# A hybrid decoder trunk on one core: the top-k mixer's probabilities transposed in 32-blocks on VectorE and carried by transfers, instead of 128-blocks on TensorE

## The chip, the core and the metric

The kernel runs on one core of a Trainium2 chip. The metric is the device time of one execution in microseconds (us). Three runs of the kernel before took 1161.17 to 1161.87 us, median 1161.53.

## What is computed

Two layers over a sequence of 512 tokens, 1024 features wide, all in float32. Each layer normalises x, scales and shifts it by a conditioning vector (`mod = silu(c) @ w_ada + b_ada`), projects it with one wide matrix (`z = u @ w_in`), runs three token mixers on parts of z, gates their outputs, projects each back, sums them and adds the result to x:

```
ya = dsa_attention(rope(aq), rope(ak), av, rope(iq), rope(ik), iw)   # "a": top-k attention, 8 heads of 64
yb = swa_sinks_attention(rope(bq), rope(bk), bv, sinks)              # "b": window of 128, 8 query heads, 2 key heads
yc = stick_breaking_attention(cq, ck, cv)                            # "c": 8 heads of 64
merged = sum over b of sigmoid(m_b) * ((y_b * silu(gate_b)) @ w_br_b)
x = x + gate * (merged @ w_out)
```

Mixer a scores all earlier keys with a small indexer, keeps the 128 highest for each query, and takes a softmax of `q k / 8` over those alone: `p = softmax(logits where selected)`, `y = p @ v`. The kernel computes all causal logits and adds a mask of -1e30 where a key is not selected.

## The kernel before, in words

**Layout.** Activations lie feature-major: 128 features on the partitions, 512 tokens along the row. Weights stream from HBM in chunks of 128x512 (256 KB) into `wstage` (4 buffers, lines 706 to 751); each chunk is split into a high part `whi` and a rest `wlo` (a cast and a subtraction, on VectorE, ScalarE or GpSimd), and every product is three matmuls (`uh*whi`, `ul*whi`, `uh*wlo`). One projected tile of 128 features takes 24 of them into one PSUM bank (`ttile`, line 981); there are three such banks (`ps_z`) and five others (`ps_s`).

**Mixers.** Heads go in pairs p = 0 to 3, two heads e to a pair, the 512 queries in four blocks i of 128. For mixer a the steps of a pair are:

- `softmax_qk` (line 1240): logits of the causal blocks into five PSUM banks; VectorE adds the mask and takes the row maximum, writing five `t` buffers of 128x512; ScalarE takes the exponent with the row sum in `den`; then each of the eight (e, i) stretches of 128 to 512 columns is multiplied in place by 1/den, on VectorE or ScalarE (line 1305).
- `softmax_tr` (line 1309): P has queries on the partitions, and the product with V needs keys there. TensorE transposes the 20 causal blocks of 128x128 one by one into five PSUM banks (line 1326), and each bank is copied to another `t` buffer by ScalarE or VectorE (line 1331).
- `softmax_pv` and `value_run` (lines 1335 to 1357): for key block j and head e, V (64 columns) is the weight and the transposed stretch of up to 512 columns is the moving operand; the two heads use the two halves of the array. `finish_pair` (line 1144) multiplies by the gate and splits y into high part and rest.

Mixers b and c use the same steps with 14 and 20 blocks. `RIDE` and `GROUPS` (lines 47, 48) say where the product with V goes: for mixer a, pair 0 goes with the logits of pair 1, pairs 1 and 2 go together after the transposes of pair 2, and pair 3 goes alone.

**Order.** `Weave` (line 81) lays out a first order of all streams, with fixed distances (`SPACE`, line 43; 13.022 us in mixer a from the logits to the transposes of a pair, 0.5 us from there to the product with V). `Recorder` (line 261) then simulates the engines with a price for each instruction (`price`, line 337), lets each instruction go as soon as its operands and buffers are there, picks the engine where there is a choice, and repeats this five times with priorities from the latest allowed start; the best order is emitted as it stands. So every engine, and SP's queue of transfers, runs a fixed order, and an instruction that is late holds up what stands behind it. Beside the mixers runs the filling work: tiles of the projection (`ttile`) and of the branch projections (`branch_item`, line 1419), the latter adding up k = 0 to 3 over the pairs' y. Mixer a is the last of the three; when its pair 3 is under way only the `ma` gate tiles and the first three parts of a branch tile can still go without pair 3's y.

**Buffers.** `SLOTS` (line 152) gives 14 buffers of 128x512 to `t`; `vc`, `vb` and `va` (V of the three mixers) have one buffer each; x and the merged result reuse `vc` and `va`. All transfers but eight are issued by SP; the eight saves of x are issued by ScalarE (line 1502).

Of the kernel before, what the change touches and what calls it, by code (L numbers as in the profile page):

```python
# [25 lines left out]
F32 = mybir.dt.float32  # L26
# [6 lines left out]
S = 512  # L33
P = 128
# [9 lines left out]
QCOST = 2408  # L44
BKEY = "cfree2"
LOAD_AHEAD, SPLIT_AHEAD = 4, 3
RIDE = {('c', 1): (0,), ('c', 2): (1,), ('c', 3): (2,), ('a', 1): (0,)}
GROUPS = {'c': ((3,),), 'a': ((1, 2), (3,)), 'b': ((0, 1), (2, 3))}

# [74 lines left out]
def by_tile(wv, *gens):  # L124
# [6 lines left out]
    while live:  # L131
# [15 lines left out]
        else:  # L147
# [1 line left out]

SLOTS = {"t": 14, "e": 2, "zs": 2, "m2": 2, "zc": 2, "G": 2, "sm": 2, "Y": 5, "Q": 2, "KH": 2, "dot": 2, "dotg": 2,
         "m8": 2, "mx": 2, "nm": 2, "den": 2, "wstage": 4, "whi": 4, "wlo": 4, "ps_z": 3, "ps_s": 5}


# [9 lines left out]
class View:  # L165
# [14 lines left out]
    def rearrange(self, how, a):  # L180
# [2 lines left out]
        at = np.lib.stride_tricks.as_strided(self.at, (n, a, w // a), (self.at.strides[0], self.at.strides[1] * (w // a), self.at.strides[1]))  # L183
        return View(self.tile, self.ops + (("rearrange", how, a),), at, self.dtype)

    def unsqueeze(self, d):
        return self._with(np.expand_dims(self.at, d), self.dtype, "unsqueeze", d)

# [7 lines left out]
    def real(self):  # L196
        ap = self.tile.real()
        for name, arg, *more in self.ops:
            ap = ap.rearrange(arg, a=more[0]) if more else getattr(ap, name)(arg)
        return ap  # L200

    def regions(self):
# [58 lines left out]
class Recorder:  # L261
# [75 lines left out]
    def price(self, x, engine, op, args, kw):  # L337
# [16 lines left out]
        from_psum = any(v.tile.pool.name[:3] == "ps_" for v in x.reads)  # L354
        if engine == "PE":
            if op == "pairs":
                w = [q[2].shape[-1] for q in args]
# [52 lines left out]
    def forward(self):  # L410
# [38 lines left out]
        while len(out) < len(self.list):  # L449
# [51 lines left out]
            if y.mode == "dma":  # L501
                if not x.writes:
                    x.end = at + 2.1
                else:
                    x.end = dma_free = max(at + (2.1 if at < 20.0 else 3.0), dma_free) + y.lag * (1.2 if dma_free < 5.5 else 1.0)
# [121 lines left out]
def trunk(ctx, tc, xT, vecs, w_ss, w_gt, w_first, w_t, w_v, w_br, w_o, rope, consts, out):  # L627
# [272 lines left out]
    def key_and_value(z):  # L900

        zs, m2, zc = t512("zs"), t512("m2"), t512("zc")
        cast(zs, z)
        cast(zc[H0], z[H0])
        SP.dma_start(zc[H1], zs[H0])
        for a, b in ((0, 32), (32, 0), (64, 32), (96, 0)):
            SP.dma_start(m2[a:a + 32], zs[b:b + 32])
        both(zc, zc, cos_t, OP.mult)
        both(m2, m2, sin_t, OP.mult)
        both(zc, zc, m2, OP.add)  # L910
        tb = sbank()
# [328 lines left out]
    def softmax_qk(b, p):  # L1240
        def fn():
# [8 lines left out]
            es = (0, 1)  # L1250
# [34 lines left out]
            for e in range(2):  # L1285
# [14 lines left out]
                DVE.reciprocal(den[:, es], den[:, es])  # L1300
                for i in (3, 2, 1, 0):
                    bk, c0 = pos(e, i)
                    t = pt[bk][:, c0:c0 + keys(b, i)[1]]
                    r = den[:, 4 * e + i:4 * e + i + 1]
                    rec.add({"DVE": ("tensor_scalar", (t, t, r, None), dict(op0=OP.mult)), "ACT": ("activation", (t, t, AF.Copy), dict(scale=r))})
            st["p", p] = pt
        return op(1900 if b == "a" else 1400, fn)

    def softmax_tr(b, p):
        def fn():  # L1310
            pt = st.pop(("p", p))
            pos, tpos = (bpos, btpos) if b == "b" else (apos, cpos)
# [5 lines left out]
            for e in range(2):  # L1318
                for j in range(4):
                    bk, c0 = tpos(e, j)  # L1320
                    if tb[bk] is None:
                        tb[bk] = sbank()
                    for i in (range(j, min(4, j + 2)) if b == "b" else range(j, 4)):
                        sbk, s0 = pos(e, i)
                        kc = s0 + 128 * j - keys(b, i)[0]
                        PE.transpose(tb[bk][:, c0 + 128 * (i - j):c0 + 128 * (i - j) + 128], pt[sbk][:, kc:kc + 128], ident)
                    left[bk] -= 1
                    if not left[bk]:
                        W = 384 if b == "b" and bk >= 2 else 512
# [5 lines left out]
    def value_run(b, ps, bank, quads=()):  # L1335

        quads, ys = list(quads), []
        for p in ps:
# [4 lines left out]
            for j in range(4):  # L1343
                W = min(256, S - 128 * j) if b == "b" else S - 128 * j
                for e in range(2):
                    bk, c0 = tpos(e, j)
                    h = 2 * p + e
                    c = 64 * (h // 4 if b == "b" else h)
                    quads.append((y[64 * e:64 * e + 64, 128 * j:128 * j + W], st["v" + b][:, j, c:c + 64], PT[bk][:, c0:c0 + W], j == 0))
        pairs(quads)  # L1350
        for p, y in ys:
            finish_pair(b, p, y)
# [66 lines left out]
    def branch_item(l, b, d):  # L1419
        def fn(w):  # L1420
# [15 lines left out]
            both(g, g, s, OP.add)  # L1436
            if b == "a":
                if d % 4 == 0:
                    st["mh", d // 4] = rec.tile(("vc", "va")[d // 4], [P, 4, S], F32R)
# [117 lines left out]
    def start():  # L1557
# [18 lines left out]
        xx = [rec.tile(t, [P, 4, S], F32) for t in ("vc", "va")]  # L1576
# [151 lines left out]
```

## Time and profile before

| | |
|---|---|
| median of the runs | 1161.53 us |
| the profiled execution's own time | 1161.48 us |
| its span, first to last instruction | 1159.7 us |
| TensorE busy | 1148.5 us, 99% of the span |
| VectorE, ScalarE, GpSimd busy | 965.7, 550.9, 170.4 us |
| moved by the DMA engines | 139.39 MB, mean 120 GB/s |
| granted TensorE clock, mean | 0.998 |

The profile page has one busy total for each engine, the span cut into 40 slices, the chain of waits that ended last followed back from the end, and groups of like instructions. All recorded instructions carry the line of the helper that emits them (599, or 597 for the pairs of matmuls in half arrays), so a group is told by its tiles: `ps_s<-small,t` is a transpose of a `t` buffer against the identity (`small` holds it), `t<-ps_s` the copy out of PSUM, `m<-zs` the swap of halves for the rotary embedding. Matmuls overlap, so the distance of their starts, and not the duration of one, is what TensorE spends; the chain of waits gives that.

### The profile page before, as it was taken

Reading aid. Unit: us, or ns where it says so; the run is one execution under the profiler, and the core shown is the slowest. Engines: PE = TensorE matmul, PEld = TensorE weight load, DVE = VectorE, ACT = ScalarE, POOL = GpSimd, SP = SyncE. Lnnn points to the kernel's source line nnn. Section 1 sums busy time; section 2 is a strip of 40 time slices with the busy share of each in tenths; the row PEclk is TensorE's granted clock in tenths of the full one; section 3 lists DMA queues with packets and bytes.
Section 4 is the critical chain, followed back from the end, with each engine's and each line's share of the span. In section 5 each row is a group of like instructions: output and inputs, shape, how many; then the busy total and the mean of one; then the engine's idle time right before and its main releaser. Section 6 shows DMA issues by size and latency. Waiting matters only on the chain.

```text
span 1159.7 us, 17599 instructions
## 1 busy us (share of the span) xinstructions
PE 1148.5 (99%) x5891; PEld 960.7 (83%) x5891; DVE 965.7 (83%) x2222; ACT 550.9 (48%) x1165; POOL 170.4 (15%) x221
## 2 busy tenths in 40 slices
PE   8999999999999999999999999999999999999997
PEld 6899887888888887788899988778888888877886
DVE  8967999999898986877687589999998988567765
ACT  5623676753565642432133157674545665232222
POOL 0100355511011100000000015562010010000001
PEclk9999999999999999999999999999999999999999
DMA  9744333344344355346534432334333333223343
GB/s 355 230 118 123 92 84 92 108 118 114 110 111 122 121 149 141 100 128 181 168 115 110 124 108 75 99 91 121 108 100 105 98 90 109 91 82 92 96 123 108
DMA packets 80474, 139.39 MB, mean 120 GB/s; under 512 B 9984, under 2 KB 20480, under 8 KB 80384
## 3 DMA queue, kind: packets, MB, share of 16 engines
q1 hardware_dynamic: 79232, 136.17, 40.4%
q10 hardware_dynamic: 1152, 2.10, 0.5%
q8 instruction: 46, 0.75, 0.3%
q14 instruction: 44, 0.36, 0.1%
HBM read 125.39 MB, written 4.19 MB: 112 GB/s over the span
## 4 chain that ended last, share of the span: by engine, by line
PE 98%; DVE 1%; ACT 0%; DMA 0%; issue 0%; SPq 0%; DVEq 0%
PE ps_z L599 74%; PE ps_s L599 18%; PE ps_s L597 4%; PE ps_z L597 2%; DMA vc<-in_xT 0%; ACT t L599 0%; DVE t L599 0%; DVE Y L599 0%; DVE wlo L599 0%; DVE xm L599 0%; ACT csr L599 0%; ACT zs L599 0%; ACT e L599 0%; DVE whi L599 0%; ACT ps_s L599 0%
## 5 line engine op out<-in xcount | busy, mean ns | idle before, releaser
L599 PE MATMUL ps_z<-uh,whi 128*128 128x512 f32 (+1 forms) x905 | 355.4, 394 | 0.0
L599 PE MATMUL ps_z<-uh,wlo 128*128 128x512 f32 (+1 forms) x905 | 352.2, 390 | 0.0
L599 PE MATMUL ps_z<-ul,whi 128*128 128x512 f32 (+1 forms) x905 | 352.0, 390 | 0.0
L599 DVE TENSOR_TENSOR wlo<-wstage,whi 128x512 fp32r<-128x512 f32 (+2 forms) x292 | 190.9, 657 | 16.2 <-ACT whi L599 6.7
L599 PEld LDWEIGHTS ps_z<-uh,wlo 128*128 128x128 f32 x905 | 170.0, 188 | 34.8 <-issue 0.5
L599 PEld LDWEIGHTS ps_z<-uh,whi 128*128 128x128 f32 x905 | 169.9, 188 | 34.8 <-issue 1.9
L599 PEld LDWEIGHTS ps_z<-ul,whi 128*128 128x128 f32 x905 | 170.0, 188 | 33.0 <-issue 0.3
L599 DVE CAST whi<-wstage 128x512 fp32r<-128x512 f32 (+1 forms) x202 | 82.7, 410 | 122.4 <-PE ps_z L599 101.4
L599 POOL TENSOR_TENSOR wlo<-wstage,whi 128x512 fp32r<-128x512 f32 (+1 forms) x80 | 102.3, 1283 | 367.3 <-ACT whi L599 133.7
L599 ACT CAST whi<-wstage 128x512 fp32r<-128x512 f32 (+2 forms) x129 | 77.2, 603 | 128.5 <-PE ps_z L599 107.2
L599 PE MATMUL ps_z<-Y,whi 128*128 128x512 f32 x384 | 119.2, 391 | 0.0
L599 ACT ACTIVATE e<-ps_z 128x512 f32<-128x512 f32 x68 | 40.4, 594 | 116.9 <-PE ps_z L599 116.6
L599 PEld LDWEIGHTS ps_z<-Y,whi 128*128 128x128 f32 x384 | 71.7, 188 | 14.5
L599 ACT ACTIVATE e<-e 128x512 f32<-128x512 f32 x96 | 59.8, 630 | 34.5 <-DVE e L599 33.8
L599 PE MATMUL ps_z<-Y,wlo 128*128 128x512 f32 x192 | 74.9, 390 | 0.0
L599 ACT ACTIVATE t<-t 128x512 f32<-128x512 f32 x120 | 69.3, 625 | 8.9 <-DVE t L599 8.5
L599 ACT ACTIVATE t<-t,nm 128x256 f32<-128x256 f32 (+3 forms) x128 | 65.1, 510 | 11.5 <-DVE nm L599 11.4
L599 PE MATMUL ps_s<-small,t 128*128 128x128 f32 x432 | 57.3, 273 | 0.0
L599 PEld LDWEIGHTS ps_s<-small,t 128*128 128x128 f32 x432 | 50.2, 140 | 7.8 <-ACT t L599 1.6
L599 DVE MAX8 m<-score 128x8 f32<-128x256 f32 (+2 forms) x96 | 53.1, 555 | 1.3
L599 DVE MATCH_REPLACE8 score<-m,score 128x256 f32<-128x256 f32 (+2 forms) x96 | 52.1, 543 | 0.1
L599 PE MATMUL ps_s<-wlo,uh 128*128 128x364 f32 x144 | 47.5, 330 | 0.0
(218 smaller groups left out, 1950.6 us busy)
## 6 DMA issues: line engine op xcount, KB each, us to landing
wstage<-in_w_t SPq DMA_DIRECT2D x212, 256.0 KB, 2.7
wstage<-in_w_v SPq DMA_DIRECT2D x48, 182.0 KB, 2.4
m<-zs SPq DMA_DIRECT2D x128, 64.0 KB, 2.0
wstage<-in_w_gt SPq DMA_DIRECT2D x32, 256.0 KB, 2.7
wstage<-in_w_ss SPq DMA_DIRECT2D x32, 256.0 KB, 2.8
wstage<-in_w_o SPq DMA_DIRECT2D x32, 256.0 KB, 2.7
Y<-in_w_ss SPq DMA_DIRECT2D x15, 512.0 KB, 5.8
wstage<-in_w_first SPq DMA_DIRECT2D x16, 256.0 KB, 3.9
```

The lines of the kernel that those rows point to most:

```text
L597: self.real[engine].matmul(*[real(a) for a in q[:3]], start=q[3], stop=True, skip_group_check=True)
L599: made = getattr(self.real[engine], y.op)(*[real(a) for a in y.args], **{k: real(v) for k, v in y.kw.items()})
```

## The change

For mixer a alone (`TR32`), the multiplication by 1/den writes to a new tile `X` of 128x2560 instead of back into `t`. X holds the 20 blocks as four quarters of 640 columns: quarter b has the 32 columns 32b to 32b+31 of every block, so a written stretch falls into runs of 32. VectorE then transposes every 32x32 square of a quarter in place (one instruction of 128x640, four to a pair). After that, square (a, b) of each block holds the right values but sits on partitions 32a instead of 32b; 16 transfers of 32x640 (80 KB) for each pair carry it from X to `U`, issued by SP or ScalarE as the planner picks. The product with V reads its moving operand from U in runs of 32 columns. TensorE's transposes of mixer a and the copies from PSUM go; mixers b and c keep theirs, but their copies now go to one tile `U` of 128x2560.

Buffers: `t` has 5 instead of 14; X and U have one each; `vc` and `vb` become one tile `V5` of 128x2560, whose room also takes the transposed P of pairs 1 and 3 of mixers a and b. Prices: a transfer from SBUF to SBUF now costs SP or ScalarE 0.63 us and another 0.35 (before: 0.58 and 0.36 on SP, 0.1 on ScalarE), and a small one lands after 2.2 instead of 3.0 us.

```diff
+TR32 = {'a': (0, 1, 2, 3)}
-SLOTS = {"t": 14, "e": 2, ...
+SLOTS = {"t": 5, "X": 1, "U": 1, "e": 2, ...
@@ price
-            y.cost, y.lag, y.mode = (0.58 if x.reads and x.writes and not x.reads[0].tile.pool.fixed else 0.36) if engine == "SP" else 0.1, n * 4 / 385e3, "dma"
+            y.cost, y.lag, y.mode = (0.63 if x.reads and x.writes and not x.reads[0].tile.pool.fixed and not o.tile.pool.fixed else 0.35) if engine == "SP" else 1.0 if engine == "POOL" else 0.63 if x.reads and not o.tile.pool.fixed else 0.35, n * 4 / 385e3, "dma"
@@ forward
-                    x.end = dma_free = max(at + (2.1 if at < 20.0 else 3.0), dma_free) + ...
+                    x.end = dma_free = max(at + (2.1 if at < 20.0 else 2.2 if y.lag < 0.22 else 3.0), dma_free) + ...
@@ key_and_value
-        v = st["vb"] = rec.tile("vb", [P, 4, P], F32)
+        st["V5"] = rec.tile("V5", [P, 5 * S], F32)
+        v = st["vb"] = st["V5"][:, 4 * S:].rearrange("p (a b) -> p a b", a=4)
@@ v_phase
-            st["vc"] = rec.tile("vc", [P, 4, S], F32)
+            st["vc"] = st["V5"][:, :4 * S].rearrange("p (a b) -> p a b", a=4)
@@ softmax_qk
-                    t = pt[bk][:, c0:c0 + keys(b, i)[1]]
+                    W = keys(b, i)[1]
+                    t = o = pt[bk][:, c0:c0 + W]
+                    if p in TR32.get(b, ()):
+                        if X is None:
+                            X = rec.tile("X", [P, blocks(b) * P], F32)
+                        o, t = strided(X, b, e, i), t.split((W // P, 4, 32), (0, 1, 2))
-                    rec.add({"DVE": ("tensor_scalar", (t, t, r, None), dict(op0=OP.mult)), "ACT": ...
+                    rec.add({"DVE": ("tensor_scalar", (o, t, r, None), dict(op0=OP.mult)), "ACT": ...
+    def softmax_tr32(b, p):
+        def fn():
+            pt = st.pop(("p", p))
...
+            N = blocks(b)
+            X = pt
+            U = st["V5"][:, :N * P] if p % 2 and b in ('a', 'b') else rec.tile("U", [P, N * P], F32)
+            n = N * 32
+            for b_ in range(4):
+                q = X[:, n * b_:n * b_ + n]
+                DVE.transpose(q, q)
+                for a_ in range(4):
+                    how = ("dma_start", (U[32 * b_:32 * b_ + 32, n * a_:n * a_ + n], X[32 * a_:32 * a_ + 32, n * b_:n * b_ + n]), {})
+                    rec.add({"SP": how, "ACT": how})
+            st["pt", p] = U
@@ softmax_tr (mixers b and c)
-                        PT[bk] = t512("t", 10)
+                        if all(v is None for v in PT):
+                            whole = st["V5"] if b != "c" and p % 2 else rec.tile("U", [P, 5 * S], F32)
+                        PT[bk] = whole[:, S * bk:S * bk + S]
@@ value_run
+                    if p in TR32.get(b, ()):
+                        lo = column(b, e, j)
+                        x = PT.split((4, blocks(b), 32), (1, 0, 2))[:, lo:lo + W // P]
+                        o = o.split((W // P, 4, 32), (0, 1, 2))
+                    else:
+                        x = PT[bk][:, c0:c0 + W]
```

## Rows read from the trace of the kernel before

**Rows 1.** The page: busy time of each engine, then two of the lines of 40 slices (VectorE's busy tenths, and TensorE's granted clock in tenths).
```profile
PE 1148.5 (99%) x5891; PEld 960.7 (83%) x5891; DVE 965.7 (83%) x2222; ACT 550.9 (48%) x1165; POOL 170.4 (15%) x221
...
DVE  8967999999898986877687589999998988567765
...
PEclk9999999999999999999999999999999999999999
```

**Rows 2.** The page: the chain of waits that ended last, by engine.
```profile
PE 98%; DVE 1%; ACT 0%; DMA 0%; issue 0%; SPq 0%; DVEq 0%
```

**Rows 3.** The page's groups: all 128x128 transposes of the three mixers (count, busy us, mean ns of one).
```profile
L599 PE MATMUL ps_s<-small,t 128*128 128x128 f32 x432 | 57.3, 273 | 0.0
```

**Rows 4.** The chain of waits in order of time, first layer, mixer a (start us, us, what, count). `ps_s L599 x20` and the two `x10` are transposes, `L597` x16 and x32 the products with V, `ps_z L599` projection work.
```profile
341.51 16.54 PE ps_z L599 x72
358.05 2.18 PE ps_s L599 x20
...
367.88 2.31 PE ps_z L597 x16
...
386.76 2.18 PE ps_s L599 x20
...
413.13 2.18 PE ps_s L599 x20
...
456.15 4.46 PE ps_s L597 x32
...
474.10 1.09 PE ps_s L599 x10
...
476.58 1.09 PE ps_s L599 x10
...
479.53 2.31 PE ps_s L597 x16
481.83 18.38 PE ps_z L599 x80
```

**Rows 5.** The same chain, second layer: the first and the last of the five pieces of transposes of mixer a.
```profile
926.00 2.18 PE ps_s L599 x20
...
1043.84 1.09 PE ps_s L599 x10
```

**Rows 6.** Busy time by stretch, the stretches of pairs 0, 1 and 2 of mixer a in either layer (stretch: us, then busy us and count of PE, weight loads, DVE, ACT, POOL; granted clock; DMA share; GB/s).
```profile
332.00:360.00 28.00, 28.00 (x159) 22.76 (x157) 25.67 (x64) 17.93 (x40) 2.66 (x4) 1.00 0.41 116
360.00:389.00 29.00, 29.00 (x152) 23.52 (x150) 25.37 (x66) 17.76 (x42) 3.77 (x4) 1.00 0.37 110
389.00:416.00 27.00, 27.00 (x136) 22.71 (x135) 24.91 (x64) 15.64 (x37) 4.89 (x6) 1.00 0.45 134
...
900.00:928.00 28.00, 28.00 (x159) 22.91 (x157) 25.64 (x61) 17.97 (x40) 0.40 (x1) 1.00 0.36 98
928.00:957.00 29.00, 29.00 (x152) 23.51 (x151) 23.84 (x58) 18.08 (x42) 3.20 (x3) 1.00 0.32 89
957.00:984.00 27.00, 27.00 (x136) 22.72 (x135) 23.92 (x57) 16.23 (x38) 1.23 (x2) 1.00 0.38 107
```

**Rows 7.** Groups of instructions in the stretch 332 to 416 us: the copies of transposed blocks out of PSUM (count, busy us, mean ns).
```profile
L599 DVE COPY t<-ps_s 128x512 f32<-128x512 f32 x7 | 4.6, 685 | 0.0
...
L599 ACT COPY t<-ps_s 128x512 f32<-128x512 f32 x8 | 4.4, 579 | 0.0
```

**Rows 8.** Groups of the whole span by shape: VectorE instructions of several widths (count, busy us, mean ns).
```profile
L599 DVE CAST whi<-wstage 128x512 fp32r<-128x512 f32 x158 | 67.3, 427 | 93.8 <-PE ps_z L599 84.1 <-PE ps_s L599 6.5 <-issue 2.4
...
L599 DVE TENSOR_TENSOR_SCAN t<-ps_s,t 128x511 f32<-128x511 f32 x40 | 47.1, 1205 | 0.1
...
L599 DVE COPY t<-ps_s 128x512 f32<-128x512 f32 x33 | 21.7, 682 | 0.1
...
L599 DVE COPY t<-ps_s 128x384 f32<-128x384 f32 x7 | 3.8, 547 | 0.0
```

**Rows 9.** The transfers from SBUF to SBUF that exist: issue on SP's queue (ns min/median/max), and time from issue to landing.
```profile
L599 SPq DMA_DIRECT2D m<-zs x128: 507/583/1627, 55.0 to 974.1; - x128
...
DMA to landing us min/median/max: 1.9/2.0/3.5
```

**Rows 10.** The transfers that ScalarE issues: issue time (ns min/median/max).
```profile
L599 ACTq DMA_DIRECT2D xsave<-xm x8: 326/333/353, 545.1 to 584.7; - x8
```

**Rows 11.** The page's transfers: the weight chunks (count, KB each, median us from issue to landing).
```profile
wstage<-in_w_t SPq DMA_DIRECT2D x212, 256.0 KB, 2.7
```

**Rows 12.** Instructions in order of time at pair 3 of the first layer: VectorE's and ScalarE's last multiplications by 1/den, then TensorE's first matmul after the product with V, and its first one with y of pair 3.
```profile
475.71 0.67 DVE L599 TENSOR_SCALAR t<-t,den 128x384 f32<-128x384 f32 x2
...
475.25 1.02 ACT L599 ACTIVATE t<-t,den 128x512 f32<-128x512 f32 x2
...
481.76 0.50 PE L599 MATMUL ps_z<-uh,wlo 128*128 128x512 f32 x1
...
483.49 0.39 PE L599 MATMUL ps_z<-Y,whi 128*128 128x512 f32 x1
```

**Rows 13.** The same chain of waits in mixer c: the end of pair 0's transposes, and the product with V that goes with the next pair's logits.
```profile
138.06 0.44 PE ps_s L599 x4
...
142.06 2.30 PE ps_z L597 x16
```

**Rows 14.** Instructions in order of time at pair 0 of mixer a, first layer: VectorE's last multiplication by 1/den.
```profile
352.39 0.61 DVE L599 TENSOR_SCALAR t<-t,den 128x384 f32<-128x384 f32 x2
```

More of the change, by code (lines that the diff above doesn't have):

```diff
@@ L148, in by_tile @@
             yield item
-SLOTS = {"t": 14, "e": 2, "zs": 2, "m2": 2, "zc": 2, "G": 2, "sm": 2, "Y": 5, "Q": 2, "KH": 2, "dot": 2, "dotg": 2,
+SLOTS = {"t": 5, "X": 1, "U": 1, "e": 2, "zs": 2, "m2": 2, "zc": 2, "G": 2, "sm": 2, "Y": 5, "Q": 2, "KH": 2, "dot": 2, "dotg": 2,
          "m8": 2, "mx": 2, "nm": 2, "den": 2, "wstage": 4, "whi": 4, "wlo": 4, "ps_z": 3, "ps_s": 5}
@@ L184, in rearrange, with split, quarters @@
         return View(self.tile, self.ops + (("rearrange", how, a),), at, self.dtype)
+    def split(self, sizes, perm):
+        n, w = self.at.shape
+        st_, strides = self.at.strides[1], []
+        for k in range(len(sizes)):
+            strides.append(st_ * int(np.prod(sizes[k + 1:])))
+        at = np.lib.stride_tricks.as_strided(self.at, (n, *sizes), (self.at.strides[0], *strides))
+        return View(self.tile, self.ops + (("split", tuple(sizes), tuple(perm)),), at.transpose(0, *[k + 1 for k in perm]), self.dtype)
+    def quarters(self):
+        n, w = self.at.shape
+        at = np.lib.stride_tricks.as_strided(self.at, (n // 4, 4, w), (self.at.strides[0], self.at.strides[0] * (n // 4), self.at.strides[1]))
+        v = View(self.tile, self.ops + (("quarters", None),), at, self.dtype)
+        v.regions = self.regions
+        return v
     def unsqueeze(self, d):
@@ L198, in real @@
         for name, arg, *more in self.ops:
-            ap = ap.rearrange(arg, a=more[0]) if more else getattr(ap, name)(arg)
+            if name == "quarters":
+                ap = ap.rearrange("(a r) n -> r a n", a=4)
+            elif name == "split":
+                ap = ap.rearrange("p (%s) -> p %s" % (" ".join("abcd"[:len(arg)]), " ".join("abcd"[k] for k in more[0])), **dict(zip("abcd", arg)))
+            else:
+                ap = ap.rearrange(arg, a=more[0]) if more else getattr(ap, name)(arg)
         return ap
@@ L356, in price @@
             if op == "pairs":
-                w = [q[2].shape[-1] for q in args]
+                w = [int(np.prod(q[2].shape[1:])) for q in args]
                 low, full = ([v for v, q in zip(w, args) if (q[2].dtype == F32) == t][::2] for t in (False, True))
@@ L504, in forward @@
                 else:
-                    x.end = dma_free = max(at + (2.1 if at < 20.0 else 3.0), dma_free) + y.lag * (1.2 if dma_free < 5.5 else 1.0)
+                    x.end = dma_free = max(at + (2.1 if at < 20.0 else 2.2 if y.lag < 0.22 else 3.0), dma_free) + y.lag * (1.2 if dma_free < 5.5 else 1.0)
                 lanes.append(x.end)
@@ L1249, in fn @@
             den = rec.tile("den", [P, 8], F32)
-            es = (0, 1)
+            es, X = (0, 1), None
             for i in (3, 2, 0, 1) if b == "a" else (2, 3, 1, 0):
@@ L1302, in fn, with blocks, grid, strip @@
                     bk, c0 = pos(e, i)
-                    t = pt[bk][:, c0:c0 + keys(b, i)[1]]
+                    W = keys(b, i)[1]
[4 more added lines that the diff above has]
+                        o, t = strided(X, b, e, i), t.split((W // P, 4, 32), (0, 1, 2))
                     r = den[:, 4 * e + i:4 * e + i + 1]
-                    rec.add({"DVE": ("tensor_scalar", (t, t, r, None), dict(op0=OP.mult)), "ACT": ("activation", (t, t, AF.Copy), dict(scale=r))})
-            st["p", p] = pt
+                    rec.add({"DVE": ("tensor_scalar", (o, t, r, None), dict(op0=OP.mult)), "ACT": ("activation", (o, t, AF.Copy), dict(scale=r))})
+            st["p", p] = X or pt
         return op(1900 if b == "a" else 1400, fn)
+    def blocks(b):
+        return 14 if b == "b" else 20
+    def grid(X, b):
+        return X.split((4, blocks(b), 32), (1, 0, 2))
+    def strip(b, e, i):
+        if b == "b":
+            return (7 * e + 2 * i - 1, 1, 2) if i else (7 * e, 1, 1)
+        return (i, 3, i + 1) if e == 0 else (16 + i, -4, i + 1)
+    def column(b, e, j):
+        return 7 * e + 2 * j if b == "b" else 4 * j if e == 0 else 16 - 3 * j
+    def strided(X, b, e, i):
+        g0, dg, n = strip(b, e, i)
+        g = grid(X, b)
+        return g[:, g0:(g0 + dg * n if g0 + dg * n >= 0 else None):dg]
+    def softmax_tr32(b, p):
+        def fn():
+            pt = st.pop(("p", p))
+            pos = bpos if b == "b" else apos
+            N = blocks(b)
[9 more added lines that the diff above has]
+            st["pt", p] = U
+        return op(1520 if b == "b" else 2180, fn)
     def softmax_tr(b, p):
+        if p in TR32.get(b, ()):
+            return softmax_tr32(b, p)
         def fn():
@@ L1348, in value_run @@
                     c = 64 * (h // 4 if b == "b" else h)
-                    quads.append((y[64 * e:64 * e + 64, 128 * j:128 * j + W], st["v" + b][:, j, c:c + 64], PT[bk][:, c0:c0 + W], j == 0))
+                    o, x = y[64 * e:64 * e + 64, 128 * j:128 * j + W], None
+                    if p in TR32.get(b, ()):
+                        lo = column(b, e, j)
+                        x = grid(PT, b)[:, lo:lo + W // P]
+                        x = PT.split((4, blocks(b), 32), (1, 0, 2))[:, lo:lo + W // P]
+                        o = o.split((W // P, 4, 32), (0, 1, 2))
+                    else:
+                        x = PT[bk][:, c0:c0 + W]
+                    quads.append((o, st["v" + b][:, j, c:c + 64], x, j == 0))
         pairs(quads)
@@ L1438, in fn @@
                 if d % 4 == 0:
-                    st["mh", d // 4] = rec.tile(("vc", "va")[d // 4], [P, 4, S], F32R)
+                    st["mh", d // 4] = rec.tile("V5", [P, 5 * S], F32R)[:, :4 * S].rearrange("p (a b) -> p a b", a=4) if d == 0 else rec.tile("va", [P, 4, S], F32R)
                 if d % 2 == 0:
@@ L1575, in start @@
         DVE.scalar_tensor_tensor(gb, b_ada[0][:, 8:16], 1.0, g_sb[0], op0=OP.add, op1=OP.mult)
-        xx = [rec.tile(t, [P, 4, S], F32) for t in ("vc", "va")]
+        xx = [rec.tile("V5", [P, 5 * S], F32)[:, :4 * S].rearrange("p (a b) -> p a b", a=4), rec.tile("va", [P, 4, S], F32)]
         x = st["x"] = [xx[k // 4][:, k % 4] for k in range(KT)]
```

## The prediction

> **What bounds the kernel now.** I read the busy totals first, then the chain of waits, then the stretches around mixer a. TensorE is busy 1148.5 of 1159.7 us and its granted clock is in the top tenth all through [rows 1]; the chain that ends last is TensorE for 98% [rows 2]. So a microsecond of TensorE work taken away is one of the end, unless TensorE then waits. The next engine is VectorE at 83% on average, but at nine tenths in many slices [rows 1]: in the stretches of pairs 0 to 2 of mixer a it is busy 75.95 of 84 us in the first layer and 73.40 of 84 in the second, with ScalarE at 51.3 and 52.3 and GpSimd at 11.3 and 4.8 [rows 6]. Mixer a runs in TensorE's shadow except at one place. Pair 0's stretches are all normalised at 353.0 us [rows 14], its transposes stand at 358.05 and its product with V at 367.88; pairs 1 and 2 are multiplied only at 456.15 [rows 4]. Pair 3 alone is tight: normalised at 476.4 [rows 12], multiplied at 479.53 [rows 4].
>
> **What goes.** A duration of 273 ns for a transpose [rows 3] is not its price, since they overlap. The chain has the 20 transposes of a pair as one piece of 2.18 us, or two of 1.09, in both layers [rows 4, 5]: 0.109 us each, and 8 x 2.18 = 17.4 us for eight pairs. That is the gain at most, up to some tenths for the change of mode around them. The Trainium skill (TensorE: Matmul & The Clock Gate, Part 4: PE-mode transpose) gives about 275 ns for a transpose in a kernel and says that the full clock doesn't engage for them. By its figure the term would be 160 x 0.275 = 44 us (an estimate); the trace has the same duration but 0.109 us from start to start, and a granted clock of 1.00 in the stretches that hold them [rows 6], so I do not take it.
>
> The 40 copies from PSUM go too: in pairs 0 to 2 of the first layer 7 on VectorE and 8 on ScalarE, 4.6 and 4.4 us [rows 7]. None is on the chain; what they give is room.
>
> **What comes, on VectorE.** Per pair four 32-block transposes of 128x640, which no row shows. Lower end: the fast cast of 427 ns for 512 columns [rows 8], scaled to 640, 0.53 us. Upper end: the scan's 1.205 us for 511 columns [rows 8], 1.51 us. I take one element per step, as the copies from PSUM have it: 547 ns for 384 and 682 for 512 [rows 8], so 135 ns per 128 and 0.82 us for 640; less the 0.08 by which neighbours overlap there, 0.74. Four make 2.95 us a pair. The strided multiplications by 1/den keep their columns; between no cost and the loss of their fast form (2560 columns a pair, at 1.05 instead of some 0.5 ns: 1.4 us if all are VectorE's) I take none, their rows being still runs of 32.
>
> VectorE's demand in the three stretches of the first layer is then 75.95 + 3 x 2.95 - 4.6 = 80.2 us, in a time of 84 - 3 x 2.18 = 77.5: more than fits. The planner can hand normalisations and weight casts to ScalarE, which holds 51.3 - 4.4 us there plus the transfers it issues (below: 24 x 0.58 = 14), 61 of 77.5. So at least 3 us of work must move, and a little will be late: I take 1 us of TensorE idle per layer, 2 us in all; the ends are nothing, and the rival below.
>
> **What comes, on the queues.** 16 transfers of 80 KB a pair, 128 in all. The nearest rows are the rotary swaps of 64 KB: 0.58 us of issue, landed 2.0 after it began [rows 9]. Sixteen cost 9.3 us of issue on one queue, 4.7 on two. ScalarE's own issues take 0.33 [rows 10], but those go to HBM; I use 0.58 for both. For pairs 0 to 2 this is covered: from 353.0 us, 2.95 of transposes, 9.3 of issue and 2.0 of landing, even end to end, reach 367.3, the product's old place being 367.88. That cover is thin with TensorE earlier, but other projection work can go first there; pairs 1 and 2 have 40 us.
>
> **Pair 3.** Old distance from last normalisation to product: 476.4 to 479.53. New: first transpose done at 477.2; 16 issues on two queues start their last at 481.3, landed 483.3; on one queue 477.2 + 15 x 0.58 + 2.0 = 487.9. The product is 3.8 to 8.4 us later, and TensorE is there 2.2 earlier: 6.0 to 10.6 us to cover. Behind the product lie 18.4 us of projection work [rows 4], which starts at 481.76, with y needed from 483.49 [rows 12]. Of it 19 matmuls of the next gate tile at 0.23 (16.54/72, rows 4), 9 of the next branch tile and 12 of the gate tile after can go ahead, 9.2 us, if PSUM banks and weights are there. So on two queues it is covered, and on one not quite. I take 0.75 us per layer, 1.5 in all (ends: 0; 16, see the rival).
>
> **The rest, at nothing.** Five `t` buffers: mixer c's are read by its transposes until 138.5 us, and the next pair writes only after its logits, beside the product at 142.06 [rows 13]; without that gap each late pair would cost its wait. U and V5 are written by a pair's copies after the product of their earlier tenant, or late V has been read; if that order were broken the copies, and TensorE's banks behind them, would wait. Strided moving rows in the product with V: from nothing to a second pass over its 2 x (2.31 + 4.46 + 2.31) = 18.2 us [rows 4]; I take nothing, as columns and weights stay the same. The new prices make a new order everywhere; I leave that at 2 us either way.
>
> **Sum.** -17.4 + 2.0 + 1.5 = -13.9 on the profiled execution's 1161.48 us, 0.05 below the median: 1147.6.
>
> **Rivals.**
> *VectorE becomes the bound.* If little is handed over and VectorE can be filled to 95%, the six stretches need 80.2/0.95 = 84.4 and, with as many copies in the second layer, (73.40 + 8.85 - 4.6)/0.95 = 81.7 us: they gain 1.9 together instead of 13.1. With the two pairs 3 (-4.4 + 1.5) that gives -4.8, 1156.7. For it: the 90% of rows 6. Against: ScalarE's and GpSimd's idle share. The Trainium skill (VectorE: DVE Perf Modes, Rules for kernel authors) advises TensorE for a 128x128 transpose whose result may go to PSUM; that is this rival's side, and the trace speaks against the rule where TensorE is the bound, for it where VectorE is.
>
> *Pair 3 is not covered.* If only the 19 matmuls (4.3 us) can move, two queues leave 6.0 + 1.7 (from product to y) - 4.3 = 3.4 us a layer, one queue 8.0. Then -17.4 + 2 + 6.8 = -8.6, 1152.9; at worst 1162. For it: y of pair 3 gates every later branch tile. Against: the 9.2 us above.
>
> *Slower: SP's queue holds up the weights.* A burst stands in SP's fixed order in front of weight chunks, and waits there for VectorE. TensorE eats a chunk of 12 matmuls in 2.76 us [rows 4]; four ahead make 11.0, less 2.7 to land [rows 11] and 1.1 to split (0.43 for the cast and 0.68 for a subtraction at one element per step, rows 8), 7.2 of cover. If SP issues all sixteen unbroken, with 0.74 of wait, it is shut for 10.0 us: 2.8 of stall at each of eight bursts, 22.4 against 17.4, so +5.0 with nothing else: 1166.5. It decides from a shut time of 7.2 + 2.2 = 9.4 us a burst. For it: 9.3 us of issue. Against: ScalarE shares them, and the planner can put loads between.
>
> **Chances.** Forecast 0.55, VectorE 0.17, pair 3 0.13, SP's queue 0.15. About 0.2% (2.3 us) is what a measurement of this kernel tells from no change. Of the VectorE case 0.03, of pair 3 0.02 and of SP's queue 0.02 fall within that: faster 0.80, same 0.07, slower 0.13. The range: low, the whole 17.4 and 2 of the new order, 1142; high 1160.5, which takes in VectorE's case and pair 3's but for its worst. The forecast's own range is 1143 to 1151.
>
> **What would show it.** Right: no `ps_s<-small,t` of mixer a (432 down to 272), TensorE's busy time down by some 17 us, its idle time up by under 5; VectorE's transposes near 0.82 us; the products of pairs 0 to 2 free of waits. VectorE's rival: idle of TensorE on `whi` or `wlo` from VectorE in 330 to 410 and 900 to 980. Pair 3's: a gap of over 3 us before its product or before the first matmul with its y. SP's: weight loads queued behind transfers, and waits on `wstage`. I am wrong if TensorE's busy time falls by 17 and the span doesn't follow for a reason in none of these, or if the products with V lengthen.

## The result, and the profile of the changed kernel

The changed kernel takes 1145.95 us (median; 1145.84 to 1146.28) against 1161.70 (1161.17 to 1162.05) for the kernel before in the same rounds: ratio 0.9865, 95% interval 0.9848 to 0.9882. The profiled execution took 1145.84 us with a span of 1144.0, so 15.7 us of span have gone. The lines of helpers are L620 and L618 now instead of L599 and L597.

The page: busy time, two of the lines of 40 slices, and the chain by engine.
```profile
PE 1133.1 (99%) x5731; PEld 943.6 (82%) x5731; DVE 985.9 (86%) x2254; ACT 541.3 (47%) x1140; POOL 144.1 (13%) x206
...
DVE  8977999999999987887686589999999999767765
...
PEclk9999999999999999999999999999999999999999
...
PE 92%; DVE 5%; DMA 1%; issue 1%; ACT 0%; SPq 0%; DVEq 0%; ACTq 0%
```
Against [rows 1], TensorE has 160 matmuls fewer and 15.4 us less of busy time, and its clock has not moved: the span fell by what TensorE no longer does. VectorE has 20 us more and GpSimd 26 less; more of VectorE's slices stand at nine tenths. In the chain VectorE went from 1% [rows 2] to 5%.

TensorE's transposes (groups by shape: count, busy us, mean ns).
```profile
L620 PE MATMUL ps_s<-small,t 128*128 128x128 f32 x272 | 38.1, 273 | 0.1
```
What reads or writes X, by operation (ns min/median/max, first and last start); `V` is the tile V5, and the last line is for the transfers.
```profile
L620 SPq DMA_DIRECT2D U<-X x37: 507/586/1329, 356.5 to 983.2; - x37
L620 ACTq DMA_DIRECT2D V<-X x36: 514/530/689, 389.2 to 1035.8; - x36
L620 DVE STREAM_TRANSPOSE X<-X x32: 799/822/846, 355.6 to 1033.2; 128x640 f32<-128x640 f32 x32
L620 SPq DMA_DIRECT2D V<-X x28: 507/592/818, 389.2 to 1036.2; - x28
L620 ACTq DMA_DIRECT2D U<-X x27: 514/552/1529, 356.5 to 980.4; - x27
...
DMA to landing us min/median/max: 2.0/2.5/5.2
```
432 transposes [rows 3] are 272. SP issues 65 of the 128 transfers, ScalarE 63, at 0.53 to 0.59 us each.

Two stretches that answer to [rows 6] (us, then busy us and count of PE, weight loads, DVE, ACT, POOL; granted clock; DMA share; GB/s): pairs 0 to 2 in either layer.
```profile
333.00:413.00 80.00, 79.32 (x390) 63.89 (x389) 77.25 (x190) 45.85 (x105) 7.29 (x6) 1.00 0.52 155
893.00:971.00 78.00, 78.00 (x385) 62.96 (x385) 72.92 (x174) 42.93 (x98) 8.40 (x7) 1.00 0.48 135
```
VectorE went from 90% to 97% in the first layer. There, and there alone, TensorE stands for 0.68 us.

The chain of waits in order of time, first layer, mixer a; with [rows 4], what stands where the pieces of 2.18 and 1.09 us stood.
```profile
342.50 13.83 PE ps_z L620 x60
356.36 0.07 DVE X L620
...
361.60 0.84 DVE X L620
...
363.02 0.75 DVE X L620
...
365.88 0.61 DVE zc L620
...
366.53 4.15 PE ps_z L620 x17
...
371.45 2.31 PE ps_z L618 x16
...
421.92 4.46 PE ps_s L618 x32
...
460.95 19.54 PE ps_z L620 x84
480.49 2.30 PE ps_s L618 x16
482.80 17.23 PE ps_z L620 x75
```
Three things are to be seen. No piece of transposes is left, and the products with V take 2.31, 4.46 and 2.30 us as before. At 356 to 366 us the chain runs through VectorE, one instruction behind the other, all four transposes of pair 0's X among them; it ends at `zc`, a product for the rotary embedding that reads a projected tile out of PSUM, for which the next tile waited: TensorE stood 0.68 us and restarted with gaps, 0.9 in all. And pair 3 has no wait at all: one piece of projection work of 19.54 us ends where its product begins.

**Where the 15.7 us lie.** Starts of the same work in both traces: the projection block that the chain shows at 55.44 us before starts at 56.20 after, 0.76 late. Mixer a's first logits move from 339.35 to 340.33, the second layer's first block from 623.29 to 616.48, its first logits of mixer a from 907.29 to 900.62, the end from 1159.7 to 1144.0. The two stages that hold mixer a give 7.79 (from +0.98 to -6.81) and 9.03 (from -6.67 to -15.70), where four pairs of 2.18 are 8.72: the first is short by the 0.9 us of the wait, the second is 0.3 above. The stages ahead of them lose 0.98 and 0.14, most of it at the start. There, VectorE's order has changed. VectorE in order of time, the kernel before:
```profile
16.88 0.76 DVE L599 TENSOR_TENSOR ul<-e,uh 128x256 fp32r<-128x256 f32 x2
17.55 1.22 DVE L599 SCALAR_TENSOR_TENSOR Y<-Y,csr 128x1024 f32<-128x1024 f32 x1
```
The same moment in the changed kernel:
```profile
16.60 1.21 DVE L620 SCALAR_TENSOR_TENSOR Y<-Y,csr 128x1024 f32<-128x1024 f32 x1
...
17.74 0.41 DVE L620 TENSOR_TENSOR ul<-e,uh 128x256 fp32r<-128x256 f32 x1
```
The planner put a dot product of 1.2 us (`Y<-Y,csr`, for the conditioning) ahead of `ul`, and TensorE waits for `ul`, here and once more at 50.9 us: 0.16 us of idle time each, but 0.44 and 0.55 us from one start to the next where 0.12 and 0.23 are usual, together 0.64 of the 0.76.

### The profile page after: what moved, and what is told of

The parts are those of the page before. It is cut to its first block, busy times and chain, and to the rows that moved or that the text cites. A ratio compares the mean times of both kernels' runs of the same rounds, so it can differ in the third digit from the quotient of the medians.

```text
span 1144.0 us, 17545 instructions
## 1 busy us (share of the span) xinstructions
PE 1133.1 (99%) x5731; PEld 943.6 (82%) x5731; DVE 985.9 (86%) x2254; ACT 541.3 (47%) x1140; POOL 144.1 (13%) x206
## 4 chain that ended last, share of the span: by engine, by line
PE 92%; DVE 5%; DMA 1%; issue 1%; ACT 0%; SPq 0%; DVEq 0%; ACTq 0%
PE ps_z L620 71%; PE ps_s L620 15%; PE ps_s L618 4%; DVE t L620 2%; PE ps_z L618 1%; DVE wlo L620 1%; DMA Y<-in_w_ss 1%; DVE Y L620 1%; DMA wstage<-in_w_first 0%; DVE Q L620 0%; SPq L620 0%; DVE ps_s L620 0%; DVE X L620 0%; DVE V L620 0%; DVE m L620 0%
## 5 line engine op out<-in xcount | busy, mean ns | idle before, releaser
L620 PE MATMUL ps_z<-uh,whi 128*128 128x512 f32 (+1 forms) x905 | 354.2, 393 | 0.7 <-DVE zc L620 0.7
L620 PE MATMUL ps_z<-ul,whi 128*128 128x512 f32 (+1 forms) x905 | 352.5, 390 | 0.3 <-DVE ul L620 0.3
L620 PE MATMUL ps_z<-uh,wlo 128*128 128x512 f32 (+1 forms) x905 | 351.4, 389 | 0.0
L620 DVE TENSOR_TENSOR wlo<-wstage,whi 128x512 fp32r<-128x512 f32 (+2 forms) x328 | 215.7, 659 | 11.1 <-ACT whi L620 3.6
L620 PEld LDWEIGHTS ps_z<-uh,whi 128*128 128x128 f32 x905 | 169.8, 188 | 35.7 <-issue 1.4
L620 PEld LDWEIGHTS ps_z<-ul,whi 128*128 128x128 f32 x905 | 169.9, 188 | 34.3 <-issue 1.0
L620 PEld LDWEIGHTS ps_z<-uh,wlo 128*128 128x128 f32 x905 | 169.9, 188 | 34.2 <-issue 0.3
L620 DVE CAST whi<-wstage 128x512 fp32r<-128x512 f32 (+2 forms) x198 | 80.6, 408 | 86.9 <-PE ps_z L620 68.3
L620 ACT CAST whi<-wstage 128x512 fp32r<-128x512 f32 (+2 forms) x132 | 79.2, 602 | 111.6 <-PE ps_z L620 89.8
L620 PE MATMUL ps_z<-Y,whi 128*128 128x512 f32 x384 | 118.7, 390 | 0.0
L620 ACT ACTIVATE e<-ps_z 128x512 f32<-128x512 f32 x68 | 40.4, 595 | 116.9 <-PE ps_z L620 100.6
L620 ACT ACTIVATE e<-e 128x512 f32<-128x512 f32 x96 | 60.0, 630 | 54.1 <-DVE e L620 35.4
L620 PEld LDWEIGHTS ps_z<-Y,whi 128*128 128x128 f32 x384 | 71.9, 188 | 14.8
L620 ACT ACTIVATE t<-t,nm 128x256 f32<-128x256 f32 (+3 forms) x128 | 65.2, 511 | 33.0 <-DVE nm L620 32.6
L620 PE MATMUL ps_z<-Y,wlo 128*128 128x512 f32 x192 | 74.7, 389 | 0.0
L620 POOL TENSOR_TENSOR wlo<-wstage,whi 128x512 fp32r<-128x512 f32 (+2 forms) x44 | 56.1, 1275 | 141.8 <-PE ps_z L620 68.6
L620 ACT ACTIVATE t<-t 128x512 f32<-128x512 f32 x120 | 67.5, 629 | 2.1 <-DVE t L620 1.2
L620 POOL CAST whi<-wstage 128x512 fp32r<-128x512 f32 x42 | 25.8, 615 | 303.9 <-PE ps_z L620 229.0
L620 DVE MAX8 m<-score 128x8 f32<-128x384 f32 (+2 forms) x96 | 53.5, 557 | 1.5
L620 DVE MATCH_REPLACE8 score<-m,score 128x384 f32<-128x384 f32 (+2 forms) x96 | 52.0, 542 | 0.1
L620 PE MATMUL ps_s<-KH,Q 128*128 128x256 f32 (+3 forms) x280 | 48.4, 303 | 0.0
L620 PE MATMUL ps_s<-whi,ul 128*128 128x364 f32 x144 | 47.5, 330 | 0.0
```

Of the source, the lines that this page charges most:

```text
L620: made = getattr(self.real[engine], y.op)(*[real(a) for a in y.args], **{k: real(v) for k, v in y.kw.items()})
```

## The experiments

Theory 1, the forecast's: TensorE's transposes were the end, and VectorE and the queues have just enough room for what takes their place. Against it stood that buffers and prices do it, and that VectorE or a queue becomes the bound. Each time is a median with its range; all ratios are against the kernel before on the same chip. Every variant is planned anew, so its whole order can differ: the projection block that starts at 55.44 us before starts anywhere from 55.29 to 56.55 in the variants whose chain shows it.

### Buffers, tiles and prices without the transposition

```diff
-TR32 = {'a': (0, 1, 2, 3)}
+TR32 = {}
```


> The kernel after with no pair given to VectorE (all transposes back on TensorE): five t buffers, U, V5 and the new prices alone. Theory 1 (the gain is TensorE's 17.4 us, less 0.8 us that the new order costs at the start of the kernel and 0.9 us of one wait for VectorE): 1161.7 to 1163, no faster than before. Rival (the new prices or tiles give a part of the gain, which VectorE and the queues then eat): 1155 to 1160.

1162.24 us (1161.91 to 1163.2), ratio 1.0004 (0.9995 to 1.0014). The five `t` buffers, U, V5 and the new prices bring and cost nothing. From here on 1162.24 is the zero of the transposition alone: its four pairs bring 16.3 us.

### Pair 3 alone, and pairs 0 to 2 alone

```diff
-TR32 = {'a': (0, 1, 2, 3)}
+TR32 = {'a': (3,)}
```


> Only pair 3 of mixer a, in either layer, goes over VectorE and the queues; pairs 0 to 2 stay on TensorE. Theory 1 (pair 3 is covered by projection work): the restructuring alone measured 1162.2, less 2 x 2.18: 1157.3 to 1158.5. Rival pair 3 (its product comes late, 3.4 us a layer): 1160 to 1165.

1158.0 us (1157.6 to 1158.32), ratio 0.9967 (0.9954 to 0.9979): 4.24 us, of the 2 x 2.18 = 4.36 that its transposes took. Pair 3 is covered, to within 0.1 us.

```diff
-TR32 = {'a': (0, 1, 2, 3)}
+TR32 = {'a': (0, 1, 2)}
```


> The changed kernel with pairs 0 to 2 of mixer a alone transposed on VectorE; pair 3 keeps TensorE's transposes. Theory 1 (each pair gives its own piece of 2.18 us per layer, and what is lost belongs to pairs 0 to 2 and to the order at the start): 1145.95 + the 4.24 that pair 3 alone gave = 1150.2, so 1149.4 to 1151.0. Rival (pair 3's gain stands only because something else gives way for it when all four pairs are moved): under 1148.5 if the four together cost more than their parts, over 1152 if the wait of 0.9 us in the first layer grows without pair 3's move.

1150.37 us (1149.54 to 1151.55), ratio 0.9903 (0.9888 to 0.9918): 11.9 us of 6 x 2.18 = 13.1. The chain has the same walk through VectorE, 355.7 to 365.9 us, and the same wait at its end, 0.7 us for `zc`. 4.24 + 11.87 = 16.1 against 16.3 for all four: the pairs add up. Where the 1.2 us are lost is less sure, as this kernel's runs lie 2 us apart. In the profiled one, the fastest, the first layer's stage with mixer a is 5.76 us shorter than without the transposition and the second's 6.69, of 3 x 2.18 = 6.54 each: there the loss is in the first layer, where the wait is.

### No work in place of the transposes

P is written straight to U and V5; the 32-block transposes and their transfers are left out, so that the products with V are taken over P untransposed.
```diff
-                            X = rec.tile("X", [P, blocks(b) * P], F32)
+                            X = st["V5"][:, :blocks(b) * P] if p % 2 else rec.tile("U", [P, blocks(b) * P], F32)
...
-                DVE.transpose(q, q)
...
-                    rec.add({"SP": how, "ACT": how})
-            st["pt", p] = U
+            st["pt", p] = st.pop(("p", p))
```


> The kernel after without VectorE's 32 transposes and without the 128 transfers of mixer a: its product with V reads the untransposed P, so that part of the computation is left out. What is left is the ceiling of the change. Theory 1: VectorE and the queues cost 0.9 us, so 1144.0 to 1146.0. Rival (they cost several us that something else hides): 1139 to 1143.

1144.55 us, ratio 0.985 (0.9836 to 0.9865). So the transposes were worth 1162.24 - 1144.55 = 17.7 us (17.4 in the forecast), and the changed kernel, with everything that replaces them, is 1.4 us slower: 24 us of VectorE (985.9 busy against 961.8) and 128 transfers almost for nothing. By the traces some 0.5 of it is not their price but the order at the start: the block at 55.44 us starts at 55.67 here, at 56.20 in the changed kernel.

### The transfers on SP alone, on ScalarE alone

```diff
-                    rec.add({"SP": how, "ACT": how})
+                    rec.add({"SP": how})
```


> All 128 transfers on SP's queue, none on ScalarE. Theory 1 (the order puts weight loads between them, and pair 3 has enough other projection work to cover 8 us): 1145.5 to 1148. Rival SP's queue (each burst of 9.3 us shuts out the weights): 1150 to 1166, with TensorE waiting for whi or wlo after the bursts. Rival pair 3 (one queue leaves its product 4 to 8 us late in each layer): 1150 to 1160, with the idle before that product.

1157.66 us (1156.84 to 1159.65), ratio 0.9963 (0.995 to 0.9976): 11.7 us of the 16.3 are gone, and the rival of SP's queue came; no wait of TensorE stands before a product of pair 3. SP's queue in order of time, in this kernel:
```profile
390.31 0.33 SPq L620 DMA_DIRECT2D wstage<-in_w_t  x1
392.30 10.48 SPq L620 DMA_DIRECT2D V<-X  x16
402.88 2.44 SPq L620 DMA_DIRECT2D m<-zs  x4
405.42 0.53 SPq L620 DMA_DIRECT2D wstage<-in_w_t  x1
```
The same queue in the changed kernel, at the same pair:
```profile
389.19 3.61 SPq L620 DMA_DIRECT2D V<-X  x5
393.05 0.38 SPq L620 DMA_DIRECT2D wstage<-in_w_t  x1
```
With SP alone a pair's sixteen transfers go in one piece of 10.48 us, rotary swaps follow, and no weight chunk is issued between 390.31 and 405.42 us; the one issued then lands 3.0 us later, at 408.4, and is cast at 408.94. ScalarE in the same kernel, in order of time:
```profile
408.30 0.61 ACT L620 CAST Q<-zc 64x512 fp32r<-64x512 f32 x1 [1.82 <-DVE zc L620]
408.94 0.62 ACT L620 CAST whi<-wstage 128x512 fp32r<-128x512 f32 x1
```
So the chunk is not all that came late. The cast stands behind a copy for the rotary embedding that waited 1.82 us for VectorE, and VectorE had itself waited 1.24 us, until 404.48, for the last transfers of the burst to leave X. This chain ends half a microsecond after the chunk has landed; both come of the burst, and the run does not part them. TensorE in order of time:
```profile
409.61 0.79 PE L620 MATMUL ps_z<-uh,whi 128*128 128x512 f32 x1 [3.15 <-ACT whi L620]
410.20 0.63 PE L620 MATMUL ps_z<-ul,whi 128*128 128x512 f32 x1
410.63 0.63 PE L620 MATMUL ps_z<-uh,wlo 128*128 128x512 f32 x1
```
The stretch behind its wait (columns as in the two stretches above):
```profile
409.00:425.00 16.00, 14.33 (x51) 11.26 (x52) 13.42 (x24) 7.05 (x12) 0.00 (x0) 0.80 0.76 198
```
The late cast stops TensorE for 3.15 us, and behind it its matmuls start 0.43 us apart instead of 0.23. Over the whole kernel, TensorE's busy time for the same 5731 matmuls is 1136.9 us instead of 1133.1, and its idle time 19.0 instead of 10.9: 3.8 and 8.1 us, together the 11.9 by which the span is longer.

The other queue alone:
```diff
-                    rec.add({"SP": how, "ACT": how})
+                    rec.add({"ACT": how})
```


> All 128 transfers on ScalarE's queue, none on SP. With SP alone the time was 1157.7 us, TensorE waiting for weight chunks that stood behind a burst. Theory 1 (what costs there is the queue that the weights share, not the transfers): 1144.5 to 1148 without such waits, ScalarE having 34 of 80 us idle in the stretch of pairs 0 to 2. Rival (any one queue is too slow for 16 transfers, as 9 us come before a product): 1152 to 1160.

1166.7 us (1164.45 to 1169.1), ratio 1.0039 (1.0025 to 1.0053): slower than the kernel before, and outside both expectations. Theory 1 falls for this run; that one queue is too slow stands, but I had sized it too small. TensorE's waits (us in total, times, longest):
```profile
PE ps_z L620 <- ACT e L620: 8.4, 2, 4.5
PE ps_z L618 <- DMA U<-X: 5.5, 2, 3.6
```
ScalarE in order of time, behind the sixteen transfers of the first pair:
```profile
379.88 0.62 ACT L620 CAST whi<-wstage 128x512 fp32r<-128x512 f32 x1 [13.69 <-DMA U<-X]
```
ScalarE computes nothing for 13.69 us while it issues them: its evictions (`e`) come late, and the product with V waits for the last transfers. TensorE's idle time is 15.0 us longer than in the changed kernel; these two waits are 13.9 of it.

### VectorE's work made larger

Quarters 0 and 2 of each pair are transposed three times instead of once, 32 instructions more.
```diff
-                DVE.transpose(q, q)
+                for _ in range(3 if b_ % 2 == 0 else 1):
+                    DVE.transpose(q, q)
```


> Two of the four quarters of each pair are transposed three times instead of once (the data end the same): 32 more transposes of 0.82 us, 24 us more on VectorE (2.95 a pair). VectorE is busy 77.25 of 80 and 72.9 of 78 us in the stretches of pairs 0 to 2 of the kernel after, so 8.85 more don't fit in either by 6.1 and 3.8. Theory 1 (VectorE was just at its limit): 1149 to 1156, TensorE waiting for VectorE there. Rival (the planner moves as much to ScalarE and GpSimd): 1145.5 to 1148.

1157.8 us (1154.94 to 1158.72), ratio 0.9959 (0.9947 to 0.997), a little over the expected range: 32 x 0.74 = 24 us more of VectorE cost 11.9 us at the end. VectorE's busy time rose by 17.6 us; a part of its other work was moved. TensorE's longest wait is the one already seen, now twice (waits of TensorE: us in total, times, longest):
```profile
PE ps_z L620 <- DVE zc L620: 4.7, 2, 2.5
```
The first 24 us of VectorE cost 1.4 together with the queues, the next 24 cost 11.9: the changed kernel stands just short of VectorE's limit.

### The old prices

```diff
-... 0.63 ... else 0.35) if engine == "SP" else 1.0 if engine == "POOL" else 0.63 if ... else 0.35, n * 4 / 385e3, "dma"
+... 0.58 ... else 0.36) if engine == "SP" else 0.1, n * 4 / 385e3, "dma"
...
-    max(at + (2.1 if at < 20.0 else 2.2 if y.lag < 0.22 else 3.0), dma_free)
+    max(at + (2.1 if at < 20.0 else 3.0), dma_free)
```


> The kernel after with the planner's old prices: 0.1 us for a transfer issued by ScalarE (0.53 in the trace), 0.58 by SP, 3.0 us to land (2.5 in the trace). Theory 1 (the order is as good as its prices): all transfers go to ScalarE and its later work is 7 us a pair behind plan: 1149 to 1160. Rival (slack hides it): 1145 to 1148.

1180.2 us (1178.28 to 1180.96), ratio 1.0155 (1.014 to 1.017): the direction held, the size was far above it. At 0.1 us a transfer looks free on ScalarE, so the planner gives it 115 of 128. ScalarE in order of time, at the first pair:
```profile
361.88 8.28 ACTq L620 DMA_DIRECT2D U<-X  x12
370.20 0.62 ACT L620 CAST whi<-wstage 128x512 fp32r<-128x512 f32 x1 [7.98 <-DMA U<-X]
```
Twelve issues shut ScalarE for 8.3 us. TensorE's largest waits (us in total, times, longest):
```profile
PE ps_z L620 <- DVE zc L620: 12.3, 2, 6.4
```
Which of the old prices matters more was not tried apart. The same edit in instructions, planned with wrong prices, is 34 us slower than with the right ones, and slower than no change.

### Mixer b as well, with and without the work

```diff
-TR32 = {'a': (0, 1, 2, 3)}
+TR32 = {'a': (0, 1, 2, 3), 'b': (0, 1, 2, 3)}
```


> Mixer b's 112 transposes go to VectorE and the queues too (eight pieces of 1.53 us on TensorE, 12.2 us). In mixer b's stretches VectorE is busy 229.9 of 233 us in the kernel after. Theory 1 (VectorE has no room there, and what it gets more comes back as TensorE's waits): 1142 to 1150, so a third of the 12.2 us at most. Rival (the planner always finds ScalarE or GpSimd for what VectorE can't hold): 1133.5 to 1137.

1144.39 us (1144.17 to 1144.59), ratio 0.9848 (0.9834 to 0.9863): the fastest of the complete kernels, but only 1.6 us below the changed one, where mixer b's 112 transposes hold 112 x 0.109 = 12.2 us of TensorE. In the changed kernel VectorE was already at 99% in mixer b's stretches (columns as above):
```profile
214.00:334.00 120.00, 120.00 (x613) 99.28 (x613) 118.60 (x333) 61.08 (x154) 11.37 (x13) 1.00 0.40 114
781.00:894.00 113.00, 113.00 (x568) 94.28 (x566) 111.30 (x309) 57.97 (x148) 8.73 (x11) 1.00 0.39 110
```
To see whether the work put on VectorE and the queues is the reason, the same two mixers with the transposes on VectorE and the transfers left out (the edit of the third experiment with mixer b in `TR32`):

> Mixers a and b both without TensorE's transposes, the probabilities written straight to the tiles that the product with V reads; VectorE's 32-block transposes and all transfers of them are left out, so the output of both mixers is not the reference's. Mixer b has 112 blocks, 112 x 0.109 = 12.2 us of TensorE. Theory 1 (what keeps mixer b's 12.2 us from showing when it is moved as well, 1.6 gained, is VectorE's and the queues' work in its stretches): 1144.55 - 12.2 = 1132.3, so 1131 to 1135. Rival (something else in mixer b's stretches holds it: the banks, V's buffers or the order): 1140 to 1143, as with the work in.

1131.9 us (1131.52 to 1132.7), ratio 0.9746 (0.9729 to 0.9762): 12.65 us below the same kernel for mixer a alone. Without the replacement the whole of mixer b's share shows; with it 1144.39 - 1131.9 = 12.5 us go to VectorE and the queues, against 1.4 for mixer a alone.

Where they go, the two traces tell. Mixer c's first logits in half arrays start at 123.88 us with the work and at 123.05 without it, those of the second layer at 686.80 and 675.81; the spans are 1142.4 and 1129.7. So 0.8 us are lost ahead, 10.2 in the first layer and 1.7 in the second. The kernel with the work, mixer b and then mixer a of the first layer, and the same two of the second (columns as above):
```profile
215.89:347.33 131.44, 130.78 (x643) 106.32 (x643) 129.09 (x345) 63.00 (x159) 12.42 (x15) 1.00 0.50 144
347.33:483.39 136.06, 130.88 (x601) 103.78 (x601) 120.21 (x301) 61.59 (x142) 16.32 (x18) 0.99 0.55 160
...
778.83:910.05 131.22, 130.77 (x646) 106.60 (x645) 128.98 (x345) 60.98 (x154) 15.79 (x18) 1.00 0.49 139
910.05:1038.11 128.06, 127.99 (x601) 103.17 (x601) 107.38 (x247) 62.47 (x142) 16.83 (x18) 1.00 0.49 135
```
In mixer b itself VectorE is 98% busy in both layers, and TensorE stands for 0.66 and 0.45 us; the 5.18 us stand behind it, in the first layer's mixer a. The longest of these stops in three lines, one each of the timelines of ScalarE, VectorE and TensorE:
```profile
408.10 0.72 ACT L620 ACTIVATE t<-t,nm 128x512 f32<-128x512 f32 x1 [11.44 <-DMA V<-X]
...
410.42 0.18 DVE L620 RECIPROCAL den<-den 128x4 f32<-128x4 f32 x1 [2.82 <-ACT t L620]
...
420.10 0.50 PE L620 MATMUL ps_z<-uh,whi 128*128 128x512 f32 x1 [2.86 <-DVE sm L620]
```
ScalarE computes nothing for 11.44 us until it has issued eleven transfers, VectorE waits 2.82 us for ScalarE's exponents and then works without a pause, and TensorE waits 2.86 us for one of the instructions in that row. So a queue and VectorE lie in one chain; the run without both does not part them. Why the second layer, with VectorE as full in mixer b, loses so little stays open.

## Why the prediction was right

**TensorE's transposes, -17.4.** Held. The run without any replacement gives 17.7. The Trainium skill (TensorE: Matmul & The Clock Gate, Part 4: PE-mode transpose) would have made the term 44 us (an estimate) by its 275 ns, a figure for bf16 where these are float32; the runs decide for the distance of the starts, 0.109 us.

**VectorE, 2 us lost.** The 32-block transpose had no row; taken at 0.82 us from the copies of other widths, it measured 0.822. The price of late VectorE work was put at 1 us a layer; it was 0.9 in the first layer, by one wait, and none in the second, where VectorE has 72.92 busy of 78 us. That some 3 us of work would move to ScalarE and GpSimd is not what happened: over the span GpSimd has 26 us less than before and VectorE 20 more, and in the first layer's stretch of pairs 0 to 2 both others have less than in [rows 6]. VectorE did a part later: from 413 to 460 us it is busy 37.12 of 47 us, where before, from 416 to 462, it was 32.64 of 46.

**The transfers, at nothing.** Held on two queues: issue 0.53 to 0.59 us (0.58 taken). Their landing is 2.5 us in the median, where 2.0 was taken [rows 9]; none of TensorE's waits is for it.

**Pair 3, 1.5 lost.** Mis-sized: it lost 2 x 2.18 - 4.24 = 0.1. The step that was too dear is the remainder of 0.75 us a layer, taken by judgment between covered and not covered. The projection work that could go ahead covered all of it: 84 and 85 matmuls stand between pair 3's logits and its product, 50 before. The second layer (the chain in order of time):
```profile
1020.30 19.48 PE ps_z L620 x85
1039.78 2.30 PE ps_s L618 x16
```

**The rest, at nothing, 2 us either way for the new order.** The buffers, the strided rows of the products with V and the stretches in mixer c cost nothing. The new order took 0.8, at a place that I had not looked at: the start of the kernel, far from the change. It is in the bound, but the wait for `ul` was not foreseen. The run with prices and buffers alone does not have it (its block starts at 55.29 us), and those with pair 3 or pairs 0 to 2 alone have 0.1 of it (55.58, 55.55), so it is no effect of these alone; which choice of the planner led to it stays open.

So the sum, -13.9 foreseen, is -17.4 + 0.9 + 0.8 = -15.7 by the traces: two losses of the forecast came out 1.1 and 1.4 us smaller than taken, and a third, at a place not foreseen, takes 0.8 of that back. The mechanism held; that the total fits to 1.7 us is in part luck.

**The rivals.** None came, but all were near. SP's queue was priced at 1166.5 with a decision from 9.4 us of shut time; with SP alone the burst shown took 10.48 us (10.0 taken) and stopped TensorE for 3.15 (2.8 taken). That these agree is partly luck: with the rotary swaps behind the burst no chunk was issued for 14.8 us, which by the forecast's cover of 7.2 would have been a stop of 7.6, so the cover was larger than taken; and X, which the burst held, was late as well. TensorE waited for `whi` three times, 5.3 us in all, not at each of eight bursts, and the kernel took 1157.7. That a burst on one queue stops TensorE is real; in the changed kernel, where ScalarE takes half of the transfers and weight loads stand between, no such wait is seen. VectorE as the bound shows in the run with tripled quarters and, in one chain with a queue, with mixer b. The Trainium skill (VectorE: DVE Perf Modes, Rules for kernel authors) advises TensorE for a 128x128 transpose: mixer a is against it, by 16.3 us where TensorE is the bound and VectorE has room; mixer b is nearly a tie.

## What to carry to other kernels

Price an edit on the bound engine by the distance of starts in the chain, and then ask of each engine that takes the work over how much room it has in that very stretch: here the work cost 1.4 us for mixer a, where VectorE had been 90% busy, and 12.5 with mixer b's added, where it had been 99%. Look at the stretch behind as well: most of the 12.5 was lost there, and in one layer of two, so a busy share tells where to look and not how much it will cost. Count a transfer's issue as work of the engine that issues it, spread bursts over the queues that have room, and put weight loads between them. If a planner writes the order, its prices are part of the change: look for its new order over the whole kernel, not only where the edit is.

## What the runs showed of the hardware

- **A short stop costs twice.** In the kernel with SP alone, TensorE stood 3.15 us; its granted clock was 0.80 over the next 16 us and 0.50 in the first 5.3 of them, the lower of its two levels (1.2 of 2.4 GHz), and there its matmuls started 0.43 us apart. Twelve of them at 0.43 instead of 0.23 are 2.4 of the 3.8 us by which TensorE's busy time grew over that kernel, beside 8.1 us more of standing. The wait of 0.68 us in the changed kernel left the granted clock of its stretch at 1.00.
- **The queue that issues matters.** The Trainium skill (DMA: Bandwidth & Descriptors, Issuing engines are not separate DMA queues) says that issuing from several engines only saves sequencer time, which is usually small next to the transfer. Here an issue of 0.59 us stands beside 2.5 us to land, which agrees for one transfer; but bursts of sixteen add up, and with all 128 on one engine the kernel is 11.7 us slower on SP and 20.8 on ScalarE than with both.
- **Moving rows in runs of 32 columns**, 640 columns apart, cost the float32 products nothing: 2.31 and 4.46 us as with rows in one run.
